# The first phase of a hybrid decoder layer on one Trainium2 core: all five engines in a written order, raw x transposed as it lands, modulation loads in one run

## The chip, the cores and the metric

The kernel runs on one core of a Trainium2 chip. Times are device microseconds (us). An execution's time is a little longer than its span, the stretch that the trace covers. The engines are TensorE (PE; PEld is its weight load), VectorE (DVE), ScalarE (ACT), GpSimd (POOL) and SyncE (SP, which here only issues DMA transfers). Each engine works through its own list of instructions in order; between engines, an instruction waits on semaphores for what it needs.

## The reference

One decoder layer for 256 prompt tokens and 8 sample tokens (264 columns), width 2048. What matters here is its beginning:

```python
mod = jax.nn.silu(c) @ p['w_ada'][l] + p['b_ada'][l]
sh1, sc1, gt1, sh2, sc2, gt2 = jnp.split(mod[:, None, :], 6, axis=-1)
h = rmsnorm(x, p['g_pre_mix'][l]) * (1.0 + sc1) + sh1
z = h @ p['w_in'][l]
(z_uv, hq, hf, hi, hg, gq, gk, gv, gr, glr, z_gate) = jnp.split(z, offsets, axis=-1)
```

`c` has nine rows: one of the prompt and one for each sample token, so the shift `sh1` and the scale `sc1` differ by token. The parts of `z` then feed a gated MLP branch, two gated linear recurrences (one with lower bounds computed from `hg_lb` by exponential and logarithms), a merge, an output product and a squared-ReLU MLP. All weights and data are fp32.

## The kernel before, in words

**Products.** A product of two fp32 tiles is made from three products in a rounded format: each operand is split into a high part `hi` (a cast) and a low part `lo` (operand minus `hi`), and hi·hi, hi·lo and lo·hi are summed in PSUM (lines L602, L603, L604 for the weight products). So each weight tile costs a cast on ACT (`split`, L109, giving `whi`) and a subtraction on DVE (L106, giving `wlo`), and so does each tile of activations.

**The first phase.** `h` lies transposed, 128 channels to a tile, 16 such tiles (k). Tile k needs the rows of `mod` for its channels, which are themselves products over `w_ada`. The phase therefore goes through k in five chunks, `CHUNKS = (2, 2, 4, 4, 4)`, and for each chunk through 20 groups of 256 output channels of `w_in`; partial sums lie in SBUF and each chunk adds to them. The work is cut into granules of 24 weight products with one weight load of 512 KB: in the first two chunks of k a granule has two k and 512 channels, hence two PSUM accumulators (tile `mm`); in the others four k, 256 channels and one accumulator. That makes granules 0 to 9, 10 to 19, 20 to 39, 40 to 59 and 60 to 79. There are two `mm` buffers.

At the end of each granule the accumulators are emptied: in chunk 0 by a copy (`S.copy`, on ACT, L755), later by an addition on DVE (`add`, L103).

**The weight stream.** `granule` takes the next item of `stream`, issues the 24 products, and then calls `stream.ahead()`: this splits the weights of the granule three ahead (two halves: cast, subtraction, cast, subtraction) and starts loads further ahead. Raw weights have four buffers (`RAW_BUFS`, tile `raw`; some pairs use a second kind, `araw`). Split weights have six (`SPLIT_BUFS`, tiles `whi`, `wlo`), two for each granule, so the split of granule g+3 goes into the buffers of granule g. The evictions of the accumulators stand in the program behind the call of `granule`, that is behind this split.

**Modulation.** `First(k0, n)` makes the rows for one chunk: `load` brings batches of `w_ada`; `steps` issues their products (tile `ada`, L274, batches of four in a row); `sums` copies the result (L278); `rows` transposes it (L285), adds the bias (L103) and makes the factor `A1` (L463); then `modulate` makes the tiles (`V.tensor_scalar` L414 or an ACT instruction L416, two small instructions for the 8 sample columns, a cast and a subtraction). The generator `paced` spreads this over the granules of the chunk before.

**The start.** x arrives as two blocks of 128 tokens, in two halves each. `norm_rows` sums the squares, `scale_rows` multiplies the blocks by each token's factor (on ACT and DVE, tokens lie on partitions), and `x_transposed` transposes groups of four 128x128 pieces on TensorE (L241): two groups before the first product, six more between the granules of chunk 0. The lower bounds are written far below in the program.

**Who sets the order.** Between `manual_schedule` and its exit, PE, SP and POOL keep the order in which the code is written. DVE and ACT are ordered by a scheduler from its own estimates.

Of the kernel before, what the change touches and what calls it, by code (L numbers as in the profile page):

```python
# [19 lines left out]
NS = 8  # L20
# [37 lines left out]
def hybrid_step_kernel(  # L58
# [53 lines left out]
    order = tc.manual_schedule(engines={mybir.EngineType.PE, mybir.EngineType.SP, mybir.EngineType.Pool})  # L112
# [103 lines left out]
    def norm_rows(x, xs, xsn, r):  # L216

        ss = tmp([P, 2, 2], "ss0", 1)
        rr = tmp([P, 2 + NS], "rr0", 1)
        junk = blk([P, 1024])  # L220
        for t in range(2):
            for hf in range(2):
                S.activation(junk, x[t][hf], AF.Square, accum_out=ss[:, hf, t:t + 1])
        sq = tmp([P, KT, NS], "sqs", 1)
        mul(sq, xs, xs)
        fold(sq, KT)
        ps = sum_partitions(sq, NS)
        add(ss[:, 0], ss[:, 0], ss[:, 1])
        rstd_small([ss[:, 0], ps], 1.0 / D, rr)
        V.tensor_copy(r, rr[:, 0:2])  # L230
        V.tensor_copy(xx0[:, 0:2], ss[:, 0])
        V.tensor_copy(xx0[:, 2:2 + NS], ps)
        mul(xsn, xs, rr[:, 2:2 + NS].unsqueeze(1).to_broadcast([P, KT, NS]))

    def transposed(x, k):

        ps = sm([P, 2, NP])
        hf, c0 = k // 8, (k % 8) * P
        for i in range(2):
            for t in range(2):  # L240
                T.transpose(ps[:, i, t * P:(t + 1) * P], x[t][hf][:, c0 + i * P:c0 + (i + 1) * P], ident)  # L241
        return ps

    def scale_rows(x, r):
        for hf in range(2):
# [8 lines left out]
    rx = tmp([P, 2], "rx", 1)  # L254
    norm_rows(xt, xsT, xsn, rx)
    xT = []

    def x_transposed(k):

        if k % 4 == 0:  # L260
            xT.append(blk())
        ps = transposed(xt, k)
        dst = xT[k // 4][:, k % 4:k % 4 + 2, 0:NP]
        if k % 4 == 0:
            S.copy(dst, ps)
        else:
            V.tensor_copy(dst, ps)


# [153 lines left out]

    class First:


        def __init__(self, k0, n):
            self.k0, self.n, self.kn = k0, n, 4 // n
            self.nb = KT // self.kn
            self.acc = pada.tile([P, 512], F32, tag="ada", name=nm("ada"))  # L430
            self.w = {}
# [9 lines left out]
        def steps(self, b):  # L441
            w = self.w.pop(b)
            for i in range(self.kn):
                ada_step(self.acc, b * self.kn + i, w[:, i], self.n * 64)
# [4 lines left out]
        def rows(self):  # L449
# [4 lines left out]
            for i in range(ni):  # L454
                for r in range(2):
# [14 lines left out]
            yield  # L470
            for k in range(k0, k0 + n, 2):
                js = slice(k % 4, k % 4 + 2)
                b = xT[q][:, js, :]
                modulate(b, b[:, :, 0:NP], xsn, k, 2, A1, mod[:, 0:KT, :], hh[q][:, js, :], hl[q][:, js, :])
                yield

        def paced(self, count):

            end = count - (5 if count > 9 else 1) - ADA_LEAD
            at = [b * end // self.nb for b in range(self.nb)]  # L480
            b0 = g = 0
            while b0 < self.nb:
                for b in range(self.nb):
                    if at[b] == g:
                        self.load(b)
                if at[b0 + ADA_BATCH - 1] + ADA_LEAD <= g:
                    for b in range(b0, b0 + ADA_BATCH):
                        self.steps(b)
                    b0 += ADA_BATCH
                if b0 == self.nb:  # L490
                    self.sums()
                g += 1
                yield
            yield from self.rows()
# [202 lines left out]
    uT, vF = [blk(), blk()], [blk(), blk()]  # L697
    HQ, HF, HI = ([blk(), blk()] for _ in range(3))
    begin = []
    for g in range(4):  # L700
        begin.append((g * CW, pair(uT[g // 2], g % 2), AF.Gelu_apprx_tanh))
    for g in range(4):
        begin.append((BW + g * CW, pair(vF[g // 2], g % 2), AF.Gelu_apprx_tanh))
    for i in range(2):
        for base, dst, fn in ((2048, HQ, AF.Silu), (3072, HF, None), (4096, HI, None)):
            for g in range(2):
                begin.append((base + 512 * i + g * CW, pair(dst[i], g), fn))
# [15 lines left out]
    first = First(0, CHUNKS[0])  # L723
# [8 lines left out]
    scale_rows(xt, rx)  # L732
    x_transposed(0)
    x_transposed(2)
    for b in (4, 5):
        first.steps(b)
    small_vectors()
    for b in (6, 7):
        first.steps(b)
    first.sums()  # L740
    run(first.rows())
    k0 = 0
    for ci, n in enumerate(CHUNKS):
        final = ci == len(CHUNKS) - 1
        gn = 4 // n
        ng = len(begin) // gn
        if not final:
            nxt = First(k0 + n, CHUNKS[ci + 1]).paced(ng)
        for gi in range(ng):
            accs = [new_acc() for _ in range(gn)]  # L750
            granule(win, 0, n, begin[gi * gn][0], gn * CW, accs, hH, hL, k0, True, True)
            for acc, (c0, dst, fn) in zip(accs, begin[gi * gn:gi * gn + gn]):
                z = acc[:, :, 0:NT]
                if ci == 0:
                    S.copy(dst, z)  # L755
# [4 lines left out]
            if ci == 0 and 2 * gi + 4 < KT:  # L760
                x_transposed(2 * gi + 4)
            if not final:
                next(nxt, None)
            else:
# [5 lines left out]
        if not final:  # L770
            run(nxt)
        k0 += n
    order.__exit__(None, None, None)
# [129 lines left out]
    lnlb, lnom, dlt, oml = (const([P, 8], n) for n in ("lnlb", "lnom", "dlt", "oml"))  # L903

    def lower_bounds():

        lt = [tmp([P, 8], f"lb{i}", 1) for i in range(4)]
        sub(lt[0], lbrawT, lbrawT)
        S.activation(lt[0], lt[0], AF.Exp)
        V.reciprocal(lt[1], lt[0])  # L910
        mul(lt[0], lt[0], lt[1])
        sub(lt[1], lt[0], lt[0])
        V.tensor_scalar(lt[1], lt[1], 0.0, None, ALU.max)
        V.tensor_scalar(lt[2], lt[1], 0.0, -1.0e30, ALU.is_equal, ALU.mult)
        V.tensor_scalar(lt[3], lt[1], 1.0e-19, None, ALU.max)
        S.activation(lnlb, lt[3], AF.Ln)
        add(lnlb, lnlb, lt[2])
        V.tensor_scalar(oml, lt[1], -1.0, 1.0, ALU.mult, ALU.add)
        V.tensor_scalar(lt[3], oml, 1.0e-19, None, ALU.max)
        S.activation(lnom, lt[3], AF.Ln)  # L920
        sub(dlt, lnom, lnlb)

# [19 lines left out]
    def hg_group(i):  # L942
# [8 lines left out]
        def gates():  # L951
            if i == 0:
                lower_bounds()
# [866 lines left out]
```

## Time and profile before

| | |
|---|---|
| median of 3 runs | 1940.19 us (1938.92 to 1940.46) |
| profiled execution | 1938.0 us, span 1935.8 us |
| TensorE busy | 1900.1 us, 98% of the span |
| VectorE, ScalarE, GpSimd busy | 1188.7, 1005.7, 88.0 us |
| mean granted TensorE clock | 0.995 |
| DMA | 442 MB, mean 228 GB/s |

In the rows of the timeline and of the groups, an operation is written as output<-input by the program's names, with its size, its count (x) and in square brackets the idle time of the engine before it and what ended that wait. A row of the view by stretches gives, for each engine, the busy time and the number of instructions (in the order PE, PEld, DVE, ACT, POOL), then the granted clock, the share of DMA engines that were busy, and GB/s.

### The profile page before, as it was taken

To read this page: it belongs to the slowest core of one execution; us is meant where nothing else is said; L and a number is where in the kernel's file an instruction comes from. 1 tells how busy PE (TensorE), PEld (TensorE's weight loads), DVE (VectorE), ACT (ScalarE), POOL (GpSimd) and SP (SyncE) were. 2 spreads that over 40 slices of the span, in tenths; PEclk is the share of its full clock that TensorE was granted. 3 is DMA by queue.
4 is the path that set the end of the run, shared out by engine and by line. 5 is a ranking of instruction groups with operands and counts; after the bars stand their busy time and mean duration, and the time that the engine had idled before them with its cause. 6 is when DMAs were issued, how large, how long until landed. Compare 5 with 4: busy or idle time off the path is not lost. (4 is left out here: it accounts for less than half of the span.)

```text
span 1935.8 us, 42323 instructions
## 1 busy us (share of the span) xinstructions
PE 1900.1 (98%) x17072; PEld 1810.3 (94%) x17072; DVE 1188.7 (61%) x2114; ACT 1005.7 (52%) x1827; POOL 88.0 (5%) x144
## 2 busy tenths in 40 slices
PE   6999999999999999999999999999999999999998
PEld 5989999998999998999999989999999999999997
DVE  4566667686577695565555666545556555555565
ACT  5444354665666765544444566454444545454444
POOL 1000000001101112200000010000000000000000
PEclk9999999999999999999999999999999999999999
DMA  9897787688588788987777846776565555555552
GB/s 314 299 341 250 246 285 216 212 259 277 182 268 280 220 261 277 312 262 250 253 256 231 304 138 191 226 243 191 180 184 178 184 179 181 183 178 185 179 181 100
DMA packets 339381, 442.06 MB, mean 228 GB/s; under 512 B 14931, under 2 KB 281025, under 8 KB 339185
## 3 DMA queue, kind: packets, MB, share of 16 engines
q1 hardware_dynamic: 329120, 409.62, 65.5%
q0 software_dynamic: 8992, 28.48, 4.6%
q8 instruction: 134, 2.20, 0.4%
q10 hardware_dynamic: 1072, 1.25, 0.2%
q14 instruction: 63, 0.51, 0.1%
HBM read 427.60 MB, written 11.70 MB: 227 GB/s over the span
## 5 line engine op out<-in xcount | busy, mean ns | idle before, releaser
L602 PE MATMUL mm<-b,whi 128*128 128x264 f32 x4592 | 1317.2, 287 | 7.6 <-ACT b L109 3.5
L603 PE MATMUL mm<-b,whi 128*128 128x264 f32 x4592 | 1308.6, 285 | 1.9 <-DVE b L106 1.0
L604 PE MATMUL mm<-b,wlo 128*128 128x264 f32 x4592 | 1305.3, 284 | 0.3 <-DVE wlo L106 0.2
L106 DVE TENSOR_TENSOR wlo<-raw,whi 128x512 fp32r<-128x512 f32 x1136 | 776.0, 690 | 570.0 <-ACT whi L109 567.4
L109 ACT CAST whi<-raw 128x512 fp32r<-128x512 f32 x1134 | 693.9, 618 | 726.7 <-PE mm L603 647.9
L602 PEld LDWEIGHTS mm<-b,whi 128*128 128x128 f32 x4592 | 865.8, 189 | 50.2 <-issue 23.8
L603 PEld LDWEIGHTS mm<-b,whi 128*128 128x128 f32 x4592 | 865.8, 189 | 2.6 <-DVE b L106 1.1
L604 PEld LDWEIGHTS mm<-b,wlo 128*128 128x128 f32 x4592 | 866.3, 189 | 1.4 <-DVE wlo L106 0.9
L103 DVE TENSOR_TENSOR b<-b,mm 128x528 f32<-128x528 f32 (+1 forms) x137 | 95.6, 699 | 42.3 <-PE mm L604 42.3
L1057 DVE SCALAR_TENSOR_TENSOR st<-vbc,b,st 128x128 f32<-128x128 f32 (+1 forms) x96 | 34.2, 391 | 52.3 <-DMA vbc<-vs_d 46.8
L1055 ACT ACTIVATE st<-st,fs 128x128 f32<-128x128 f32 (+1 forms) x96 | 37.0, 430 | 51.3 <-DMA st<-in_state_hgrn_dram 26.0
L274 PE MATMUL ada<-b,cT 128*32 128x256 f32 (+1 forms) x640 | 35.4, 361 | 7.4 <-DMA b<-in_w_ada_dram 7.3
L342 PE MATMUL ada<-araw,cT 128*32 128x512 f32 x296 | 39.9, 601 | 0.0
L274 PEld LDWEIGHTS ada<-b,cT 128*32 128x32 f32 x640 | 18.3, 116 | 19.5 <-issue 6.8
L100 DVE TENSOR_TENSOR b<-b,b 128x512 f32<-128x512 f32 (+1 forms) x47 | 34.2, 742 | 1.4 <-ACT b L1165 0.9
L1058 POOL DMA_DIRECT2D out_dram<-st x32 | 23.5, 735 | 153.1 <-DVE st L1057 152.3
L342 PE MATMUL ada<-b,cT 128*32 128x512 f32 x216 | 25.8, 593 | 0.0
L106 DVE TENSOR_TENSOR b<-gt,b 128x528 fp32r<-128x528 f32 x32 | 22.7, 709 | 3.7 <-ACT whi L109 0.5
L106 DVE TENSOR_TENSOR b<-b 128x1024 f32<-128x1024 f32 (+1 forms) x24 | 24.4, 1018 | 0.0
L109 ACT CAST whi<-araw 128x512 fp32r<-128x512 f32 x20 | 12.4, 621 | 20.6 <-PE mm L603 18.1
L100 DVE TENSOR_TENSOR gt<-vt 128x528 f32<-128x528 f32 x32 | 22.4, 701 | 0.9 <-ACT vt L1679 0.9
L1685 ACT ACTIVATE b<-vt 128x528 fp32r<-128x528 f32 x32 | 20.7, 647 | 1.0
(374 smaller groups left out, 872.0 us busy)
## 6 DMA issues: line engine op xcount, KB each, us to landing
raw<-in_w_in_dram SPq DMA_DIRECT2D x232, 512.0 KB, 4.6
raw<-in_w_mlp_up_dram SPq DMA_DIRECT2D x128, 512.0 KB, 3.7
raw<-in_w_mlp_down_dram SPq DMA_DIRECT2D x128, 512.0 KB, 3.6
b<-in_w_ada_dram SPq DMA_DIRECT2D x102, 512.0 KB, 6.5
araw<-in_w_ada_dram SPq DMA_DIRECT2D x74, 512.0 KB, 5.4
raw<-in_w_branch_dram SPq DMA_DIRECT2D x48, 512.0 KB, 4.4
raw<-in_w_out_dram SPq DMA_DIRECT2D x32, 512.0 KB, 4.1
b<-in_w_ada_dram SPq DMA_DIRECT2D x32, 256.0 KB, 5.9
```

Source lines behind the costliest of these rows:

```text
L100: V.tensor_tensor(o, a, b, op=ALU.mult)
L103: V.tensor_tensor(o, a, b, op=ALU.add)
L106: V.tensor_tensor(o, a, b, op=ALU.subtract)
L109: S.copy(hi, src)
L274: T.matmul(acc[32 * j:32 * j + 32, 0:n], cT[:, k, :], w[:, n * j:n * j + n], start=k == 0, stop=k == KT - 1)
L342: T.matmul(self.acc[32 * j:32 * j + 32, :], cT[:, k, :], ws[j // 2][:, j % 2 * 512:j % 2 * 512 + 512], start=k == 0, stop=k == KT - 1)
L602: T.matmul(o, a, xh(k + j), start=first and j == 0, stop=False)
L603: T.matmul(o, a, xl(k + j), start=False, stop=False)
L604: T.matmul(o, b, xh(k + j), start=False, stop=last and j == n - 1)
L1055: S.activation(st[:, i, :], st[:, i, :], AF.Copy, scale=fs[:, h0 + i, b:b + 1])
L1057: V.scalar_tensor_tensor(st[:, i, :], v[:, i, :], k[:, h0 + i, NP + b:NP + b + 1], st[:, i, :], ALU.mult, ALU.add)
L1058: nc.gpsimd.dma_start(G.s_out(b, h0, nh), st)
```

## The change

The change rewrites the first phase so that DVE and ACT, too, keep the written order. In detail:

- The list of engines in `manual_schedule` gains DVE and ACT.
- Raw x is transposed block by block as it lands (`x_block`, 32 transposes, all ahead of the first product). The token factors come later: two products of a matrix of ones with a diagonal matrix of factors spread them over all partitions (`row_factors`), and four DVE products 128x1024 scale the transposed x.
- The lower bounds move to behind granule 24, the constants of the later phases (two loads, 0.42 MB) to behind granule 22. Where these loads were, three batches of the second chunk's `w_ada` stand (six loads of 256 KB).
- The generator `paced` goes. A table says behind which granule each batch of products, the sums, the rows and each pair of tiles stand: batches of four behind granules 4 and 7; 9, 11, 14, 17; 25, 28, 31, 34; 45, 48, 51, 54; the rows and first tiles one granule after the last batch. The `w_ada` loads are spread over the granules.
- In chunk 0 the second accumulator is copied by DVE, the first by ACT (both L815).
- At the first tile (`modulate_first`) POOL makes the sample columns and DVE all prompt columns; POOL also makes the first weight subtraction.
- Blocks for the results are taken when they are first written.

```diff
-    order = tc.manual_schedule(engines={mybir.EngineType.PE, mybir.EngineType.SP, mybir.EngineType.Pool})
+    order = tc.manual_schedule(engines={mybir.EngineType.PE, mybir.EngineType.SP, mybir.EngineType.Pool, mybir.EngineType.DVE, mybir.EngineType.Activation})
...
-    norm_rows(xt, xsT, xsn, rx)
...
-        ps = transposed(xt, k)
...
-    def scale_rows(x, r):
-        for hf in range(2):
-            S.activation(x[0][hf], x[0][hf], AF.Copy, scale=r[:, 0:1])
-            V.tensor_scalar(x[1][hf], x[1][hf], r[:, 1:2], None, ALU.mult)
...
+    def x_block(t, hf):
+        S.activation(junk, xt[t][hf], AF.Square, accum_out=ss0[:, hf, t:t + 1])
+        for q in (2 * hf, 2 * hf + 1):
...
+            for j in range(4):
+                c0 = (4 * (q % 2) + j) * P
+                T.transpose(ps[:, j, :], xt[t][hf][:, c0:c0 + P], ident)
...
+    for t in range(2):
+        V.tensor_scalar(dg[:, t, 0:P], ident, rr0[:, t:t + 1], None, ALU.mult)
...
+    def row_factors():
+        ps = sm([P, 2, P])
+        for t in range(2):
+            T.matmul(ps[:, t, :], ones, dg[:, t, 0:P], start=True, stop=True)
+        rb = tmp([P, 2, NT], "vt")
+        S.copy(rb[:, 0, 0:NP].rearrange("p (t n) -> p t n", t=2), ps)
+        for q in range(4):
+            x = xT[q][:, :, 0:NP]
+            mul(x, x, rb[:, 0:1, 0:NP].to_broadcast([P, 4, NP]))
...
+    def modulate_first(b, xs, A, B, hi, lo):
+        d = b[:, :, NP:NT]
+        G = nc.gpsimd
+        G.tensor_tensor(d, xs[:, 0:2, :], A[:, 0:2, 1:NC], op=ALU.mult)
+        G.tensor_tensor(d, d, B[:, 0:2, 1:NC], op=ALU.add)
...
-    def paced(self, count):
...
-    nc.sync.dma_start(cst[:, 256:904], consts[:, 256:904])
-    nc.sync.dma_start(msk, masks.rearrange("p (l t) -> p l t", l=6))
-    for b in range(4):
+    for b in range(3):
+        firsts[1].load(b)
...
+    raw, hi, lo = halves[0]
+    nc.gpsimd.tensor_tensor(lo, raw, hi.bitcast(F32), op=ALU.subtract)
+    first.rows()
+    first.tiles(0)
...
+    at_batches(1, (4, 7))
+    at_batches(2, (9, 11, 14, 17))
...
+    at(22, rest)
+    at(24, lower_bounds)
...
                 if ci == 0:
-                    S.copy(dst, z)
+                    (V.tensor_copy if a else S.copy)(dst, z)
                 else:
                     add(dst, dst, z)
...
-            if ci == 0 and 2 * gi + 4 < KT:
-                x_transposed(2 * gi + 4)
...
+            for fn, args in acts.pop(gg, ()):
+                fn(*args)
```

What this does to the order on three engines (`mm_`, `b_`, `raw_`, `whi_` and `wlo_` with a number are single buffers in their turn):

ACT in chunk 0, between the first granules, before. `L755` copies an accumulator `mm`, `L109` casts a half of a later granule's weights, `L265` copies transposed x:

```order
L109 CAST whi_426<-raw_341 128x512
L109 CAST whi_430<-raw_341 128x512
L755 COPY b_167<-mm_400 128x528
L755 COPY b_167<-mm_401 128x528
L109 CAST whi_482<-raw_343 128x512
L109 CAST whi_486<-raw_343 128x512
L755 COPY b_168<-mm_456 128x528
L755 COPY b_168<-mm_457 128x528
L265 COPY b_494<-sm_495 128x2x256
L755 COPY b_169<-mm_501 128x528
L109 CAST whi_527<-raw_377 128x512
L109 CAST whi_531<-raw_377 128x512
```

And now, in the same place:

```order
L109 CAST whi_416<-raw_386 128x512
L109 CAST whi_420<-raw_386 128x512
L815 COPY b_426<-mm_368 128x528
L109 CAST whi_458<-raw_388 128x512
L109 CAST whi_462<-raw_388 128x512
L815 COPY b_468<-mm_432 128x528
L109 CAST whi_500<-raw_390 128x512
L109 CAST whi_504<-raw_390 128x512
L815 COPY b_510<-mm_474 128x528
```

Before, two casts stood ahead of the copies in the first granules, and later the copy of the first accumulator stood ahead of the casts; now two casts stand ahead of the copy in each granule, and one of the two copies has gone to DVE.

DVE in chunk 1 before, where `L103` adds an accumulator to the sums and `L106` subtracts for a later granule's weights:

```order
L103 TENSOR_TENSOR b_166<-b_166,mm_864 128x528
L106 TENSOR_TENSOR wlo_891<-raw_783,whi_890 128x512
L103 TENSOR_TENSOR b_166<-b_166,mm_865 128x528
L106 TENSOR_TENSOR wlo_895<-raw_783,whi_894 128x512
L103 TENSOR_TENSOR b_167<-b_167,mm_918 128x528
L106 TENSOR_TENSOR wlo_945<-raw_821,whi_944 128x512
L103 TENSOR_TENSOR b_167<-b_167,mm_919 128x528
L106 TENSOR_TENSOR wlo_949<-raw_821,whi_948 128x512
```

And now:

```order
L106 TENSOR_TENSOR wlo_933<-raw_751,whi_932 128x512
L106 TENSOR_TENSOR wlo_937<-raw_751,whi_936 128x512
L103 TENSOR_TENSOR b_426<-b_426,mm_906 128x528
L103 TENSOR_TENSOR b_426<-b_426,mm_907 128x528
L106 TENSOR_TENSOR wlo_973<-raw_828,whi_972 128x512
L106 TENSOR_TENSOR wlo_977<-raw_828,whi_976 128x512
L103 TENSOR_TENSOR b_468<-b_468,mm_946 128x528
L103 TENSOR_TENSOR b_468<-b_468,mm_947 128x528
```

The adds stood alternately with the subtractions and now stand in pairs behind both.

ACT at the start before, from the copy of the first transposed x to the casts of the first tile (`lb`, `lnlb`, `lnom`: the lower bounds; `gt`: the modulation sums):

```order
L265 COPY b_245<-sm_246 128x2x256
L909 ACT_TABLE_LOAD
L909 ACTIVATE lb_815_4677<-lb_815_4677 128x8
L278 COPY gt_295<-ada_176 128x128
L916 ACT_TABLE_LOAD
L916 ACTIVATE lnlb<-lb_818_4680 128x8
L920 ACTIVATE lnom<-lb_818_4680 128x8
L416 ACTIVATE b_245<-b_245,mod,A_165 128x256
L109 CAST whi_315<-raw_201 128x512
L109 CAST b_302<-b_245 128x264 x2
```

And now:

```order
L266 COPY vt_292<-sm_289 128x256
L279 COPY gt_343<-ada_264 128x128
L761 CAST whi_345<-raw_249 128x512
L761 CAST whi_348<-raw_249 128x512
L109 CAST b_357<-b_143 128x264 x2
```

The lower bounds with their table loads and ACT's share of the first tile are gone from here, and both weight casts stand ahead of the first tile's. POOL has this in the same place, where it had nothing (`L429` and `L430` make the sample columns):

```order
L764 ISA
L764 TENSOR_TENSOR wlo_346<-raw_249,whi_345 128x512
L429 TENSOR_TENSOR b_143<-xsn_128,A_220 128x2x8
L430 TENSOR_TENSOR b_143<-b_143,mod 128x2x8
L1024 DMA b_3866<-in_gla_w_up_dram 16x512
```

The sample columns stand behind the weight subtraction on POOL.

More of the change, by code (lines that the diff above doesn't have):

```diff
@@ L422, in hybrid_step_kernel @@
     A1 = const([P, KT, NC], "A1")
+    def modulate_first(b, xs, A, B, hi, lo):
[3 more added lines that the diff above has]
+        G.tensor_tensor(d, d, B[:, 0:2, 1:NC], op=ALU.add)
+        for j in range(2):
+            V.tensor_scalar(b[:, j, 0:NP], b[:, j, 0:NP], A[:, j, 0:1], B[:, j, 0:1], ALU.mult, ALU.add)
+        for j in range(2):
+            split(b[:, j, :], hi[:, j, :], lo[:, j, :])
     class First:
@@ L429, in __init__ @@
             self.nb = KT // self.kn
-            self.acc = pada.tile([P, 512], F32, tag="ada", name=nm("ada"))
+            self.acc = None
             self.w = {}
@@ L441, in steps @@
         def steps(self, b):
+            if b == 0:
+                self.acc = pada.tile([P, 512], F32, tag="ada", name=nm("ada"))
             w = self.w.pop(b)
@@ L454, in rows @@
             for i in range(ni):
-                for r in range(2):
+                for r in (1, 0):
                     cs = slice(r * KT + k0, r * KT + k0 + n)
@@ L469, in rows, with tiles @@
                 hl.append(blk(dt=F32R))
[L470 to L473, printed above, removed]
-                modulate(b, b[:, :, 0:NP], xsn, k, 2, A1, mod[:, 0:KT, :], hh[q][:, js, :], hl[q][:, js, :])
-                yield
-        def paced(self, count):
[L479 to L494, printed above, removed]
+        def tiles(self, k):
+            q, js = k // 4, slice(k % 4, k % 4 + 2)
+            b = xT[q][:, js, :]
+            if k == 0:
+                modulate_first(b, xsn, A1, mod[:, 0:KT, :], hh[q][:, js, :], hl[q][:, js, :])
+            else:
+                modulate(b, b[:, :, 0:NP], xsn, k, 2, A1, mod[:, 0:KT, :], hh[q][:, js, :], hl[q][:, js, :])
     rate = [0.0, 0.0]
@@ L901, in hybrid_step_kernel @@
     bg.g.append(gen_a)
[L903 to L921, printed above, removed]
     def log_sigmoid(out, z, a):
```

155 lines of the change are left out of this document (96 added, 59 removed).

## Prediction

> **What bounds the kernel now.** I read the page first, then the products by stage, then what TensorE waited for, then the timeline at the places where it waited. The page:
>
> ```profile
> span 1935.8 us, 42323 instructions
> PE 1900.1 (98%) x17072; PEld 1810.3 (94%) x17072; DVE 1188.7 (61%) x2114; ACT 1005.7 (52%) x1827; POOL 88.0 (5%) x144
> ```
>
> TensorE is the bound, so a wait of TensorE costs its full length and work taken from it is worth its full length. The change touches the time up to the end of the first 80 granules. A granule is 24 products; granules 0 to 9 (chunk 0) and 10 to 19 (chunk 1) fill two PSUM accumulators each, the later ones one. The next view counts the products (tile mm) by stage: granules 1 to 9, 10 to 19, 20 to 39, and 60 to 79.
>
> ```profile
> 34.13:68.99 34.86, 27.88 (x216) 26.83 (x217) 0.00 (x0) 10.41 (x18) 1.00 0.81 267
> 68.99:111.75 42.76, 32.71 (x242) 31.27 (x241) 13.23 (x19) 0.59 (x1) 0.96 0.99 370
> 111.75:179.20 67.45, 59.83 (x482) 58.60 (x481) 14.06 (x20) 0.00 (x0) 1.00 0.78 264
> 246.20:309.20 63.00, 59.30 (x482) 58.44 (x481) 14.07 (x20) 0.00 (x0) 1.00 0.87 285
> ```
>
> Twenty granules without trouble take 63.0 us, ten should take 31.5 and their modulation products; granules 10 to 19 take 42.76. The waits of TensorE over the whole run say what there is to gain:
>
> ```profile
> PE ada L274 <- DMA b<-in_w_ada_dram: 7.3, 3, 6.3
> PE mm L602 <- DVE b L103: 2.7, 2, 2.0
> PE mm L602 <- ACT b L755: 1.3, 2, 0.6
> ```
>
> The first is w_ada landing before there is other work. The other two are waits of a product for an accumulator to be emptied, by ACT (L755) and by DVE (L103). They are few, and the change meets just these.
>
> **Part 1: evictions behind casts, granules 1 to 9.** This is the timeline around the first ACT wait: the first product of granule 1, the casts of the weights of a later granule, the last product of granule 1, four transposes, the two copies, the first product of granule 2.
>
> ```profile
> 34.14 0.37 PE L602 MATMUL mm<-b,whi 128*128 128x264 f32 x1
> ...
> 36.51 1.35 ACT L109 CAST whi<-raw 128x512 fp32r<-128x512 f32 x2 [0.40 <-PE mm L603]
> 37.04 0.29 PE L604 MATMUL mm<-b,wlo 128*128 128x264 f32 x1
> 37.17 0.60 PE L241 MATMUL sm<-cst,b 128*128 128x128 f32 x4
> 37.77 1.09 ACT L755 COPY b<-mm 128x528 f32<-128x528 f32 x2
> 38.41 0.39 PE L602 MATMUL mm<-b,whi 128*128 128x264 f32 x1 [0.65 <-ACT b L755]
> ```
>
> The casts wait for products of the granule that runs (L603), since their buffers are that granule's: there are six, two a granule, and the split is three granules ahead. The second cast can only end about 0.7 us after the granule. ACT works in order; the copies stand behind the casts, and the next granule's first accumulator stands behind the first copy. Without the transposes TensorE could have gone on at 37.17 (0.12 after 37.04); it went on at 38.41, so this order costs 1.24 us, and here the transposes fill half of it. Before, ACT has this order in granules 1 and 2 alone; from granule 3 on the copy stands ahead. The new order has it in every granule of chunk 0: cast, cast, copy. A granule lasts 37.17 - 34.14 = 3.03, with the wait 4.27.
>
> A run of modulation products between two granules covers the wait:
>
> ```profile
> 85.62 0.28 PE L604 MATMUL mm<-b,wlo 128*128 128x264 f32 x1
> 85.84 1.93 PE L274 MATMUL ada<-b,cT 128*32 128x256 f32 x32
> 87.70 0.39 PE L602 MATMUL mm<-b,whi 128*128 128x264 f32 x1
> ...
> 90.64 0.28 PE L604 MATMUL mm<-b,wlo 128*128 128x264 f32 x1
> ```
>
> It costs 87.70 - 85.74 = 1.96, and in chunk 1 a granule lasts 90.76 - 87.70 = 3.06. After the change such runs follow granules 4, 7 and 9. From granule 1 to granule 10: 6 x 4.27 + 3 x (3.03 + 1.96) = 40.6 us, where 34.86 were: **+5.7**. The six groups of transposes that leave this stage (about 0.45 each, 2.7) are in this sum: they no longer fill the waits.
>
> **Part 2: adds behind subtractions, granules 10 to 19.** Here DVE adds both accumulators to the sums. This is the one place where before has the order that the change gives to all ten granules: cast, cast; subtraction, subtraction; add, add.
>
> ```profile
> 104.39 1.36 ACT L109 CAST whi<-raw 128x512 fp32r<-128x512 f32 x2 [1.34 <-PE mm L603]
> 104.93 0.28 PE L604 MATMUL mm<-b,wlo 128*128 128x264 f32 x1
> 105.04 1.43 DVE L106 TENSOR_TENSOR wlo<-raw,whi 128x512 fp32r<-128x512 f32 x2
> 106.39 1.31 DVE L103 TENSOR_TENSOR b<-b,mm 128x528 f32<-128x528 f32 x2
> 107.23 0.37 PE L602 MATMUL mm<-b,whi 128*128 128x264 f32 x1 [2.02 <-DVE b L103]
> ```
>
> TensorE could have gone on at 105.05 and went on at 107.23: 2.18 us. It is longer than part 1's because the second subtraction follows the second cast and the add follows it. In before's other granules the add stands between the two subtractions and no wait is seen. Now a granule takes 3.06 + 2.18 = 5.24 whether a modulation run (1.96, shorter) stands behind it or not: 10 x 5.24 = 52.4 for 42.76, **+9.6**. At granule 18 the new tiles' work, ahead of the next adds on DVE, adds some 0.5 (rows below).
>
> **Part 3: the start.** The last transpose of the modulation rows, a table load of the lower bounds, the casts of the first tile, the first product; two POOL groups of the page; the issue of the fourth weight load and its size and latency; and the DMA rate meanwhile (last number, GB/s):
>
> ```profile
> 24.58 0.33 PE L285 MATMUL sm<-cst,gt 128*128 128x128 f32 x1 [0.39 <-ACT gt L278]
> 24.55 1.28 ACT L916 ACT_TABLE_LOAD   x1
> 27.97 0.72 ACT L109 CAST b<-b 128x264 fp32r<-128x264 f32 x2
> 28.43 0.59 PE L602 MATMUL mm<-b,whi 128*128 128x264 f32 x1 [3.52 <-ACT b L109]
> ...
> L1575 POOL TENSOR_TENSOR b<-b,b 128x512 f32<-128x512 f32 x1 | 1.3, 1280 | 0.0
> L1595 POOL TENSOR_TENSOR b<-xsn,b 128x32 fp32r<-128x32 f32 x4 | 1.5, 375 | 0.3
> ...
> 22.30 0.38 SPq L562 DMA_DIRECT2D raw<-in_w_in_dram  x1
> raw<-in_w_in_dram SPq DMA_DIRECT2D x1, 512.0 KB, 7.9
> ...
> 27.00:28.00 1.00, 0.00 (x0) 0.00 (x0) 0.48 (x3) 1.00 (x3) 0.00 (x0) 0.50 1.06 401
> ```
>
> The rows are there at 24.9. The lower bounds, with a table load of 1.28 just there, leave this place, so the factor A1 can be ready at about 25.6. But POOL now makes the sample columns, and its two instructions stand behind its new weight subtraction: that needs the weight's cast (about 26.1), takes 1.28 by the 128x512 row, then twice 0.375: 28.15. One cast of 0.36 and a hand-over: first product at 28.7, where 28.43 was. The freed table load is worth nothing, since POOL's chain fills it.
>
> The fourth weight load landed at 22.30 + 7.9 = 30.2. Six batch halves of 256 KB (1.57 MB) now stand ahead of it and 0.42 MB of constants no longer: 1.15 MB more at 400 GB/s is 2.9 us, so it lands at 33.1. Its two casts stand on ACT ahead of granule 0's copy: 33.1 + 2 x 0.6 + 0.6 = 34.9, granule 1 at 34.95 for 34.14: **+0.8**. Without that lateness the order of part 1 gives the same: a granule 0 that ends at 33.7 and 1.24 more.
>
> Costed at nothing: the 32 transposes of raw x at the start, since x lands while TensorE has nothing else (its wait for w_ada above is 7.3 us) and w_ada sets the rows' time; the two products with ones, as short and as early. The four DVE products 128x1024 that scale x cost 1.02 us each by the nearest row,
>
> ```profile
> L106 DVE TENSOR_TENSOR b<-b 128x1024 f32<-128x1024 f32 (+1 forms) x24 | 24.4, 1018 | 0.0
> ```
>
> and if a broadcast operand makes one half as long again, 6 us: from about 17.7 to 23.6, still ahead of 24.9. If that cover went, the first tile would be late by the rest, 1 us at most. The lower bounds at granule 24 cost DVE some 2 us and ACT two table loads in a stage where one accumulator is filled while the other is emptied; a granule of 3 us is the slack. The constants at granule 22 and the spread w_ada loads use a DMA that is not full there (264 GB/s in the row of granules 20 to 39). SP waits, as before, for weight buffers that DVE frees; DVE's waits are for TensorE, so SP's loads slip with it and no sooner.
>
> **Part 4: tiles ahead of adds, granules 35 to 39 and 55 to 59.** Pieces of a tile, on DVE:
>
> ```profile
> 168.76 0.42 DVE L103 TENSOR_TENSOR mod<-sm,vec 128x18 f32<-128x18 f32 x4
> 170.45 0.41 DVE L414 TENSOR_SCALAR b<-b,A,mod 128x256 f32<-128x256 f32 x1
> 171.99 0.70 DVE L106 TENSOR_TENSOR b<-b,b 128x528 fp32r<-128x528 f32 x1
> ```
>
> Before, weight subtractions and adds are strewn among these. In the fixed order all of it stands between the add of granule 35 and the subtractions of the next split. From the end of granule 35: last cast and subtraction 1.46 (part 2's rows), add 0.66, rows 0.42 and 0.2, sample columns and tile 0.75, cast 0.63, subtraction 0.70: 4.9; the two subtractions of granule 39's weights and the add of granule 36: 6.9. Two granules of TensorE take 6.3 to 6.4, so granule 38 waits 0.55; the second tile pair, a granule later, makes the next wait some 1.1. Two stages: 2 x 1.7 = **+3.4**. By the same rows the smaller tiles at granules 18 and 20 cost about 0.5 each: **+1.0**.
>
> **Part 5: the clock.** What followed the wait of 2.02 us in part 2 (the last three numbers are clock, DMA share, GB/s):
>
> ```profile
> 104.00:108.00 4.00, 1.98 (x16) 1.79 (x16) 3.96 (x13) 2.24 (x4) 0.00 (x0) 1.00 0.84 273
> 108.00:111.50 3.50, 3.50 (x18) 3.50 (x17) 2.20 (x8) 1.78 (x3) 0.00 (x0) 0.51 1.03 391
> ```
>
> In the 3.5 us after it the granted clock was 0.51 and 18 products ran. The steady pace (482 products in 59.30 us, 0.123 each) gives 28.5; the 10.5 missing are 1.3 us. In chunk 1 the new order gives such a wait after every granule; runs of modulation products break three of them, seven stay. I take the clock's choice as one by fixed stretches of time in which too little ran, and a wait of 2.0 us fell there wholly into one; of seven at 5.24 us apart I let half do so: 3.5 x 1.3 = **+4.6**, with ends of 0 and 18 (each wait and the stretch after it slowed). The waits of part 1 are 1.24 and I cost them nothing: the one at 37.17 is followed by no slower product (0.39, 0.37 each at the first).
>
> [...]
>
> **The sum.** 0.8 + 5.7 + 9.6 + 1.0 + 3.4 + 4.6 = 25.1 us. All of it lies on TensorE's path ahead of granule 60; behind it the program is the same and only shifts. The profiled execution was 1938.0 (span 1935.8), 2.2 below the median of 1940.19: 1963.1 for a like execution, about **1965** for the median.
>
> **Rivals.**
>
> *The clock isn't cut by these waits.* Each wait leaves over a third of any 3.4 us stretch filled, and the slow stretch at 108.00 is one case only, so it might come of something else. Sum 20.5: about 1960.5. Chance 0.20. [...]
>
> *The clock is cut at nearly every wait.* If seven waits with both neighbouring stretches lose 2 x 1.3 each, the clock costs 18 rather than 4.6: 1979; the stretches would then be slow through all of chunk 1. Chance 0.13.
>
> *Faster.* The fixed order puts the evictions where TensorE never waits for them. The transposes (2.7), both waits seen (1.3) and the hole in granules 10 to 19 are then won: 42.76 against 10 x 3.06 and four runs of 1.96 = 38.4, 4.3 us; less 0.8 at the start, 7.5: about 1932.5. It decides whether the second cast ends 1.24 us or more before the granule's end. It would, were the split's buffers those of an earlier granule; the casts' waits on L603 in parts 1 and 2 speak against that. Chance 0.09.
>
> *No change.* Only ACT's order bites, since DVE's adds find the subtractions done: +5.7 and +0.8 less the 4.3: 1942. The row of 105.04 speaks against it. Chance 0.03.
>
> **How the numbers follow.** The main case has 0.55. Its own range is 1957 to 1975 (clock 0 to 14, tiles 0 to 5). The range has to hold 8 in 10 and so takes in the case without the clock with terms up to 8 lower, and the lower half of the case with the full clock: 1952 to 1978. A measurement of this kernel tells about 0.2% (3.9 us) from no change: faster 0.09, same 0.03, slower 0.88.
>
> **What the profile after would show.** The first product near 28.7; granule 1, 10 and 20 at 34.95, 75.5 and 128.4 (the first two sums; the third with the tiles and half of the clock's loss); the waits for ACT's copy at about 1.1 to 1.2 us a granule up to 75, those for DVE's adds at 2.0 to 2.2 up to 128; stretches of clock 0.5 in chunk 1 alone; shorter waits near granules 38, 39, 58 and 59; granule 80 at about 334 for 309.2; no transposes between the products after the first; no wait at granule 24. The prediction is wrong if the casts and subtractions of the split end well ahead of the granule's end in the new order, if the copies or adds run ahead of them, or if the waits stay and the clock does what neither end allows.

## The result, and the profile after

The changed kernel takes 1971.87 us (median of 4 runs, 1968.51 to 1975.11) where the kernel before takes 1940.33: a ratio of 1.016, 95% interval 1.0147 to 1.0173. It is slower by 31.5 us. The forecast was 1965, 1952 to 1978. The profiled execution of the changed kernel took 1974.0, its span is in the page:

```profile
span 1972.2 us, 42411 instructions
PE 1913.0 (97%) x17076; PEld 1820.9 (92%) x17076; DVE 1201.5 (61%) x2128; ACT 995.3 (50%) x1813; POOL 89.7 (5%) x147
```

The view by stretches, for granules 1 to 9, 10 to 19, 20 to 39 and 60 to 79 (all instructions, so the counts hold the modulation products too; the first number after the stretch is its length, and behind the engines stand clock, DMA share and GB/s):

```profile
35.36:75.83 40.47, 34.08 (x377) 31.03 (x377) 20.15 (x36) 17.04 (x30) 0.00 (x0) 1.00 0.88 284
75.83:133.48 57.65, 43.43 (x342) 38.55 (x339) 27.57 (x50) 14.44 (x24) 0.00 (x0) 0.88 0.61 204
133.48:203.50 70.02, 68.79 (x610) 64.15 (x611) 44.61 (x87) 30.08 (x50) 0.00 (x0) 0.98 0.74 254
271.80:334.90 63.10, 63.10 (x514) 59.17 (x513) 39.93 (x67) 32.80 (x54) 0.00 (x0) 1.00 0.89 288
```

Granules 10 to 19 stand out: TensorE is busy for 43.43 of 57.65 us, at a mean clock of 0.88, and the DMA rate is the lowest of the four, 204 GB/s, since loads wait for buffers (the load queue waited 42.8 us of the stage for weight subtractions). Stage by stage, in the two profiled executions; "behind the phase" is the time from the begin of granule 80 to the end of the last product into `mm`:

| | before | after | difference | forecast |
|---|---|---|---|---|
| granule 1 begins | 34.14 | 35.36 | +1.2 | +0.8 |
| granules 1 to 9 | 34.85 | 40.48 | +5.6 | +5.7 |
| granules 10 to 19 | 42.76 | 57.65 | +14.9 | +14.7 (9.6, 0.5, 4.6) |
| granules 20 to 39 | 67.47 | 70.04 | +2.6 | +2.2 (0.5, 1.7) |
| granules 40 to 59 | 67.04 | 68.30 | +1.3 | +1.7 |
| granules 60 to 79 | 63.01 | 63.07 | +0.1 | 0 |
| behind the phase | 1620.5 | 1630.7 | +10.2 | 0 |

The waits of TensorE over the whole run:

```profile
PE mm L599 <- DVE b L103: 15.4, 9, 2.0
PE mm L599 <- ACT b L815: 7.4, 7, 1.1
...
PE sm L630 <- issue: 2.4, 1, 2.4
PE mm L600 <- issue: 2.0, 1, 2.0
PE mm L599 <- issue: 1.8, 1, 1.8
...
PE mm L601 <- DVE wlo L106: 1.0, 1, 1.0
```

The first two rows are the forecast's: 2.7 and 1.3 us before, 15.4 and 7.4 now. The three rows with "issue", a wait for nothing that the profile shows, are new, and they lie behind the phase. So does the last, a wait for the low part of a weight (0.2 before). In chunk 0 a granule now ends like this (casts, last products, the copy, the next granule):

```profile
37.72 1.34 ACT L109 CAST whi<-raw 128x512 fp32r<-128x512 f32 x2 [2.41 <-PE mm L600]
...
38.96 0.59 ACT L815 COPY b<-mm 128x528 f32<-128x528 f32 x1
39.61 0.39 PE L599 MATMUL mm<-b,whi 128*128 128x264 f32 x1 [1.08 <-ACT b L815]
```

and in chunk 1 like this:

```profile
78.21 1.35 ACT L109 CAST whi<-raw 128x512 fp32r<-128x512 f32 x2 [3.13 <-PE mm L600]
...
78.75 0.28 PE L601 MATMUL mm<-b,wlo 128*128 128x264 f32 x1
78.86 1.43 DVE L106 TENSOR_TENSOR wlo<-raw,whi 128x512 fp32r<-128x512 f32 x2 [2.87 <-ACT whi L109]
80.21 1.31 DVE L103 TENSOR_TENSOR b<-b,mm 128x528 f32<-128x528 f32 x2
81.05 0.36 PE L599 MATMUL mm<-b,whi 128*128 128x264 f32 x1 [2.02 <-DVE b L103]
```

From 78.75 to 81.05 are 2.30 us, less the 0.12 of one product 2.18: the same chain and the same length as the one case before showed.

The clock, in five stretches of 3.4 us, laid by the two at half clock, which begin at 82.49 and 116.62 and last 3.41:

```profile
79.10:82.50 3.40, 1.45 (x12) 1.48 (x13) 2.38 (x4) 0.47 (x1) 0.00 (x0) 1.00 0.67 195
82.50:85.90 3.40, 3.40 (x23) 2.93 (x25) 0.69 (x1) 1.21 (x2) 0.00 (x0) 0.50 1.04 392
109.80:113.20 3.40, 1.97 (x16) 2.00 (x17) 1.90 (x3) 0.00 (x0) 0.00 (x0) 1.00 1.05 404
113.20:116.60 3.40, 1.38 (x11) 1.20 (x11) 2.33 (x4) 1.24 (x2) 0.00 (x0) 1.00 0.52 200
116.60:120.00 3.40, 3.40 (x17) 3.40 (x17) 0.28 (x1) 0.00 (x0) 0.00 (x0) 0.50 0.57 159
```

The wait from 78.87 to 81.05 lies in the first stretch but for 0.2 us, and the second runs at 0.50. The wait at 109 was cut by the border at 109.8, 0.7 us on one side and 1.4 on the other, and what follows runs at 1.00. The wait at 114.2 lies wholly in a stretch again, and 116.6 to 120.0 runs at 0.50.

### The profile page after: what moved, and what is told of

The parts are those of the page before. It is cut to its first block, busy times and chain, and to the rows that moved or that the text cites. A ratio compares the mean times of both kernels' runs of the same rounds, so it can differ in the third digit from the quotient of the medians.

```text
span 1972.2 us, 42411 instructions
## 1 busy us (share of the span) xinstructions
PE 1913.0 (97%) x17076; PEld 1820.9 (92%) x17076; DVE 1201.5 (61%) x2128; ACT 995.3 (50%) x1813; POOL 89.7 (5%) x147
## 5 line engine op out<-in xcount | busy, mean ns | idle before, releaser
L599 PE MATMUL mm<-b,whi 128*128 128x264 f32 x4592 | 1325.2, 289 | 28.7 <-DVE b L103 15.4
L106 DVE TENSOR_TENSOR wlo<-raw,whi 128x512 fp32r<-128x512 f32 x1135 | 775.7, 691 | 615.1 <-ACT whi L109 609.4
L109 ACT CAST whi<-raw 128x512 fp32r<-128x512 f32 x1132 | 691.6, 618 | 767.7 <-PE mm L600 694.0
L103 DVE TENSOR_TENSOR b<-b,mm 128x528 f32<-128x528 f32 (+1 forms) x137 | 94.5, 696 | 16.6 <-PE mm L601 16.6
L275 PEld LDWEIGHTS ada<-b,cT 128*32 128x32 f32 x640 | 17.4, 112 | 16.5 <-DMA b<-in_w_ada_dram 7.8
L106 DVE TENSOR_TENSOR b<-gt,b 128x528 fp32r<-128x528 f32 x32 | 22.7, 708 | 3.4
L106 DVE TENSOR_TENSOR b<-b 128x1024 f32<-128x1024 f32 (+1 forms) x24 | 24.4, 1022 | 0.0
L343 PEld LDWEIGHTS ada<-b,cT 128*32 128x32 f32 x216 | 6.9, 110 | 15.1 <-issue 14.6
```

The lines of the kernel that those rows point to most:

```text
L103: V.tensor_tensor(o, a, b, op=ALU.add)
L106: V.tensor_tensor(o, a, b, op=ALU.subtract)
L109: S.copy(hi, src)
L275: T.matmul(acc[32 * j:32 * j + 32, 0:n], cT[:, k, :], w[:, n * j:n * j + n], start=k == 0, stop=k == KT - 1)
L343: T.matmul(self.acc[32 * j:32 * j + 32, :], cT[:, k, :], ws[j // 2][:, j % 2 * 512:j % 2 * 512 + 512], start=k == 0, stop=k == KT - 1)
L599: T.matmul(o, a, xh(k + j), start=first and j == 0, stop=False)
```

## The experiments

Nine further runs were made, one of them of the changed kernel again. "Phase" is the begin of granule 80, in the profile.

**The evictions ahead of the split.** In the changed kernel, in all chunks, `granule` (its new argument is `ahead`) no longer ends with the split; the split stands behind the evictions:

```diff
-        stream[0].ahead()
+        if ahead:
+            stream[0].ahead()
...
+            late = True
+            granule(win, 0, n, begin[gi * gn][0], gn * CW, accs, hH, hL, k0, True, True, not late)
...
+            if late:
+                stream[0].ahead()
             for fn, args in acts.pop(gg, ()):
```

> The changed kernel, but in all five chunks the evictions (copies, adds) are issued ahead of the split of later weights; everything else, the fixed order too, stays. Theory A (evictions stand behind the split's casts and subtractions): the waits for L815 and L103 go; granule 10 begins near 68.5 us (now 75.8), granule 20 near 107.5 (now 133.5), granule 80 near 307 (now 334.9); the median falls by 26 to 28 to about 1944 to 1946, and by some 5 more if what the changed kernel loses behind the phase goes too. Rival B (weights or modulation rows arrive too late, whatever the order): the waits change their name but granule 20 stays later than 125, median above 1960.

Measured: 1937.23 us, ratio to before 0.9982 (0.9972 to 0.9992). The stages 1 to 9 and 10 to 19:

```profile
34.41:66.83 32.42, 32.42 (x379) 30.67 (x378) 19.23 (x35) 18.18 (x32) 0.00 (x0) 1.00 1.01 346
66.83:105.03 38.20, 35.97 (x342) 32.58 (x339) 27.14 (x50) 14.72 (x25) 0.00 (x0) 1.00 0.89 306
```

40.5 became 32.4 and 57.7 became 38.2; TensorE is busy without a gap in the first. Phase 306.5 for 334.9, and what was lost behind the phase is gone too (1620.8). Theory A holds: not the written order as such costs the time, but the place of the evictions in it. With the evictions there, the change as a whole is a small gain, 4.0 us. The time fell further than the 26 to 28, or some 33, that were expected: 34.6.

**The same in granules 10 to 19 alone.** (`late = ci == 1`.)

> The changed kernel with the evictions ahead of the split in granules 10 to 19 alone. Theory A: granules 10 to 19 take 38.5 to 39.5 us for 57.7, of which about 13 is waits and 5 to 6 the clock; the stage before it stays at 40.5; median about 1953. If the slow stretches of the clock come of something else than the waits, about 44 us and 1958. Rival B: little change.

Measured: 1951.42 us, ratio 1.0057 (1.0043 to 1.0071). Granules 1 to 9 take 40.50, granules 10 to 19 38.17 at clock 1.00. The waits and the clock of chunk 1 are thus worth 19.5 us of the phase; the forecast had 9.6 and 0.5 for the waits, 4.6 for the clock, and 4.3 for the hole of before, 19.0.

**The order alone, without the rest of the change.** The kernel before with one line:

```diff
-    order = tc.manual_schedule(engines={mybir.EngineType.PE, mybir.EngineType.SP, mybir.EngineType.Pool})
+    order = tc.manual_schedule(engines={mybir.EngineType.PE, mybir.EngineType.SP, mybir.EngineType.Pool, mybir.EngineType.DVE, mybir.EngineType.Activation})
```

> The kernel before with one line of the change: DVE and ACT are added to the engines in written order; all other code as before. Theory A (the order alone costs the time): granules 1 to 9 take about 40.5 us for 34.85, granules 10 to 19 52 to 58 for 42.8, median 1960 to 1968. Rival B (the moved loads, tiles and transposes cost it, and the order matters only with them): median below 1950.

Measured: 1968.21 us, ratio 1.0141 (1.0126 to 1.0155). Granules 1 to 9 take 40.91, granules 10 to 19 59.49 at a mean clock of 0.86:

```profile
35.63:76.54 40.91, 34.74 (x365) 32.45 (x365) 15.95 (x29) 22.99 (x43) 0.00 (x0) 1.00 0.68 227
76.54:136.03 59.49, 46.99 (x370) 41.41 (x371) 27.67 (x50) 14.84 (x25) 0.00 (x0) 0.86 0.75 272
```

So this one line makes 27.6 of the 31.5 us. Its phase ends at 337.5, 28.3 later than before's and later than the changed kernel's 334.9: inside the phase the rest of the change gains 2.6 us. The changed kernel is slower all the same, since it loses more behind the phase (1630.7 for 1622). The stage of granules 10 to 19 is longer than the 52 to 58 us expected; all six of its waits were followed by a stretch of half clock. Here the six groups of transposes still lie between the granules of chunk 0, and the stage takes as long (40.91 for 40.48): they run inside the waits.

**The rest of the change, without the order.** The changed kernel with DVE and ACT left to the scheduler (the line above in reverse).

> The changed kernel with ACT and DVE left to the scheduler again (PE, SP and POOL in written order, as before the change). Theory A: the scheduler puts most evictions ahead of the casts and alternates adds and subtractions again, so the waits go; the lower bounds stand at the start again and the first tile's casts behind all weight casts, so the first product comes at 30 to 32; granule 20 near 112, median 1945 to 1950. Rival B (the other parts of the change cost the time): median stays at 1965 or more.

Measured: 1940.57 us, ratio 0.9999 (0.999 to 1.0008). Granules 1 to 9 take 34.41, granules 10 to 19 37.48; the first product comes at 30.9 and granule 1 at 37.13, 3.0 later than before, as the lower bounds and the weights' casts stand ahead of the first tile again. Phase 307.3, 2.0 less than before; behind it the profile shows 1626.2, 5.7 more. The median is below the 1945 to 1950 that were expected, and granule 20 began at 109.0, not 112.

**The waits filled, first attempt.** To see whether the waits cost the clock, 14 products whose result is not used were put behind seven granules of chunk 1.

> The changed kernel with 14 more products, whose result is not used, behind the granules 10 to 19 that have no modulation products: they fill 1.7 of each wait of 2.2 us. Theory C (a wait of 2.2 us brings a stretch of half clock): granules 10 to 19 keep their waits for L103 but have no slow stretch, and take 52 to 53 us for 57.7; median about 1967. Rival (the slow stretches come of something else, such as the load on the power supply or the DMA): the same slow stretches, 57 to 58 us, median 1972; if the added products cost more than the waits hide, above 1972.

Measured: 1977.56 us, ratio 1.0192 (1.0178 to 1.0206); granules 10 to 19 took 67.53. The expectation was wrong, and by a slip in the experiment: the added products read a weight half, so the cast into its buffer waited for them too, and the whole chain cast, subtraction, add began later: TensorE's waits for the adds came to 16.3 us over the run, for 15.4 without the added products. It shows what the chain hangs on, the last product that reads the weights. Of the clock it says little, although it had two slow stretches in this stage.

**The waits filled, with x alone.** The same, but the added products read only tiles of x:

```diff
+        if fill:
+            ps = sm()
+            for _ in range(fill):
+                T.matmul(ps[:, 0:NT], xh(k)[:, 0:P], xh(k), start=True, stop=True)
         stream[0].ahead()
```

> As fill_c1, but the 14 unused products behind granules 10, 12, 13, 15, 16, 18 and 19 read only the tiles of x, not the weights whose buffer the next cast waits for. Theory C (a wait of about 2.2 us brings a stretch of half clock): no slow stretch in granules 10 to 19, which take 52 to 53 us for 57.7 in the changed kernel; end of the phase near 330 for 334.9. Rival (the slow stretches come of something else): four or five slow stretches as in the changed kernel and 57 to 58 us.

Measured: 1959.37 us, ratio 1.0096 (1.0083 to 1.0109). No slow stretch in granules 10 to 19:

```profile
75.85:127.67 51.82, 49.32 (x440) 44.65 (x437) 27.56 (x50) 14.46 (x24) 0.00 (x0) 1.00 0.68 228
```

With 98 products more the stage is 5.8 us shorter. The granules still begin when the adds are done (six waits for them are left, 0.3 us at most); only the clock stays, at 1.00 for 0.88. So 5.8 us of the stage were the clock's, and theory C holds here. The granules of the changed kernel say the same: those that a slow stretch met, 11, 13, 14 and 17, took 6.45, 6.71, 6.70 and 6.70 us, the other six of the stage 5.16 to 5.21, together 5.8 us more; with the waits filled all ten took 5.15 to 5.22. The phase ends at 328.7 for 334.9. The remaining gain of the median, 12.5 - 6.2 = 6.3 us, comes from behind the phase (1622.6 for 1630.7); of this below.

**POOL takes subtractions.** evict_first keeps one wait of 2.2 us, ahead of granule 20, and two slow stretches behind it. DVE there (start, duration, engine):

```profile
101.51 0.42 DVE L103 TENSOR_TENSOR mod<-sm,vec 128x18 f32<-128x18 f32 x4
102.90 0.63 ACT L109 CAST b<-b 128x528 fp32r<-128x528 f32 x1 [0.18 <-DVE b L415]
103.56 0.71 DVE L106 TENSOR_TENSOR b<-b,b 128x528 fp32r<-128x528 f32 x1 [0.74 <-ACT b L109]
104.19 1.31 DVE L103 TENSOR_TENSOR b<-b,mm 128x528 f32<-128x528 f32 x2
105.03 0.36 PE L599 MATMUL mm<-b,whi 128*128 128x264 f32 x1 [2.23 <-DVE b L103]
```

The tile of granule 18 stands ahead of the adds of granule 19. The first attempt gave POOL the weight subtractions behind granules 17 to 19.

> evict_first, and the six weight subtractions issued behind granules 17, 18 and 19 made by POOL, so that DVE reaches the adds of granule 19 sooner. Expected: the wait of 2.2 us ahead of granule 20 falls to 0.5 to 1.2 and the two slow stretches behind it go; granules 20 to 39 take 68 us for 71.2; median 1934 for 1937.2. Rival (POOL's subtractions of 1.3 us each make weights late or slow DVE): no gain or a loss, 1937 to 1942.

Measured: 1935.94 us, ratio 0.9982 (0.9972 to 0.9993), the same as evict_first's; granules 20 to 39 took 71.28 again. The expectation failed and its rival held. The rows say why:

```profile
99.13 2.54 POOL L571 TENSOR_TENSOR wlo<-raw,whi 128x512 fp32r<-128x512 f32 x2 [2.46 <-PE mm L605]
99.29 0.70 DVE L103 TENSOR_TENSOR b<-b,mm 128x528 f32<-128x528 f32 x1 [0.76 <-PE mm L606]
100.51 1.20 DVE L100 TENSOR_TENSOR b<-xsn,A 128x16 f32<-128x16 f32 x1
...
103.55 2.51 POOL L571 TENSOR_TENSOR wlo<-araw,whi 128x512 fp32r<-128x512 f32 x2 [1.88 <-ACT whi L570]
104.84 1.26 DVE L100 TENSOR_TENSOR b<-xsn,A 128x16 f32<-128x16 f32 x1
```

A DVE product of 128x16, 0.17 us in evict_first, took 1.20 and 1.26, and ended both times 0.04 us after POOL's pair of subtractions (101.67 and 106.06). The add from PSUM beside it kept its 0.70. Of what POOL took from DVE, DVE lost 1.03 us in the first of these products (1.20 for 0.17), and the wait ahead of granule 20 is 2.05 us where evict_first has 2.23. That the product waited for POOL is an estimate from these ends; how the one held up the other was not shown.

**The tile taken apart.** evict_first, with the subtraction of the tile between the two adds of granule 19, the next tile's columns there too, and the split of that granule held back:

```diff
+                if gg == 19 and a == 0:
+                    firsts[2].tiles_b(4)
+                    firsts[2].tiles_a(6)
+            if gg == 19:
+                firsts[2].tiles_b(6)
+                stream[0].hold = False
...
+            if gg == 18:
+                firsts[2].tiles_a(4)
+                stream[0].hold = True
```

> evict_first, with the first tiles of the third chunk (behind granules 18 and 19) taken apart: the subtraction of the first pair and the columns of the second stand between the two adds of granule 19, and the split of granule 21's weights waits until behind granule 19. If the 2.2 us ahead of granule 20 come of the tile's chain ahead of the adds on DVE: that wait falls below 1 us, the two slow stretches at 105 go, granules 20 to 39 take 67.5 to 68.5 us for 71.2, median about 1933. If the delayed split makes the weights of granules 21 and 22 late instead: a new wait for wlo there and no gain, 1936 to 1939.

Measured: 1932.91 us, ratio 0.9965 (0.9951 to 0.9978), the best of all. The add now comes first:

```profile
101.01 0.69 DVE L103 TENSOR_TENSOR b<-b,mm 128x528 f32<-128x528 f32 x1
101.17 0.63 ACT L502 CAST b<-b 128x528 fp32r<-128x528 f32 x1 [0.18 <-DVE b L500]
101.71 0.60 ACT L501 ACTIVATE b<-b,mod,A 128x256 f32<-128x256 f32 x1
101.84 0.71 DVE L106 TENSOR_TENSOR b<-b,b 128x528 fp32r<-128x528 f32 x1
```

The wait ahead of granule 20 is gone, two of 0.2 and 0.4 us for the tiles' low parts are left, no stretch there is slow, granules 10 to 19 take 35.81 and 20 to 39 68.45, and the phase ends at 300.8, 8.5 us before that of the kernel before. The median gains only 6.2 us, since 1623.7 us lie behind the phase, 3.2 more than before.

**The changed kernel once more,** for the loss behind the phase.

> The changed kernel once more, for a second profile. If the loss of 10 us behind the phase belongs to this program's place in memory, TensorE waits again for about 2 us near its matrix instructions 3750, 4133, 5411 and 7996 (counted from its first), each with a transfer of instructions beginning there; if it is chance, in other places or not at all. Granule 80 again near 335, median 1970 to 1974.

Measured: 1973.89 us, ratio 1.0165 (1.0147 to 1.0182), phase 335.5, and 1634.5 behind it. TensorE waits again near its instructions 3750, 4133 and 5411, for 2.60, 2.05 and 2.75 us from one instruction to the next; the fourth place shows nothing this time. In the first profile the wait at that fourth place is the one for the low part of a weight, whose subtraction ended at 852.88; the product began at 852.97. The other three have no such cause in the profile. The first of them, in the first profile of the changed kernel:

```profile
453.17 0.22 PE L630 MATMUL sm<-b 128*32 128x32 f32 x2 [2.38 <-issue]
```

and in the view of the DMA queues of those 3 us one transfer of 16 KB, on the queue that the view calls "instruction", which begins at 450.8, as TensorE stops:

```profile
q8 instruction: 1, 0.02, 2.2%
```

There are 134 such transfers in the run, and 135 in the two kernels with 98 products more. In evict_first, whose TensorE runs the same instructions in the same order, such a transfer begins 0.2 us ahead of instruction 3750, and TensorE does not wait there. Three other kernels do wait near these places; their rows, of evict_first_c1, sched_act_dve and evict_first_tiles in turn:

```profile
PE mm L600 <- issue: 3.5, 2, 2.0
PE mm L600 <- issue: 2.6, 2, 1.9
PE mm L617 <- issue: 1.1, 1, 1.1
```

Their time behind the phase, 1626.0, 1626.2 and 1623.7, is longer than before's as well. The kernels that lost little there (evict_first, evict_first_pool and the two with added products: 1620 to 1623 us) have waits of 0.5 us at most at these places or none, and order_only, with waits of about 1.2 and 1.6 at two of them, no more than 1622. The eleven profiles hold sixteen waits of 0.3 us or more that are put down to "issue". Fifteen of them end 2.2 to 2.6 us after such a transfer began, and the sixteenth 3.0 us after one that took 1.50 us and not about 1. In those fifteen the time from the transfer's begin thus varied little, while the sixteen waits were 0.3 to 2.5 us long. That the waits are for these transfers is an estimate from this timing and was not shown: no run changed the transfers. Why they begin where they do stays open.

## Why the prediction was right, and where it was not

- **Parts 1 and 2, the waits.** Right. The rows of granules that had the order before gave the price of all: 5.6 for 5.7 in chunk 0, and 2.18 us a granule in chunk 1. (That no wait is seen in before's other granules of chunk 1 was misread: one of 0.7 us, ahead of granule 18, is the second of the two in the row of 2.7.) order_only shows that the order makes them, evict_first that the place of the evictions does.
- **Part 3, the start.** The first product came at 28.43, not 28.7 (POOL's two small instructions took 0.25 each, not 0.375). Granule 1 came 1.2 later, not 0.8: the fourth weight's cast began at 33.44 on landing, 0.3 later than worked out. Granule 0, worked out to end at 33.7, ended at 34.0: it ran at half clock to its end (0.50 up to 34.7; before, up to 33.0), which the forecast did not look at. The four products that scale x took 4.63 us, 17.47 to 22.10, where up to 6 were allowed for.
- **Part 4, the tiles.** Right in size for granules 35 to 39 and 55 to 59: waits of 0.65 and 0.9 us in each of the two stages, 1.55 for 1.65. The 0.5 us at granule 18 do not show: the waits ahead of granules 19 and 20 are 1.95 and 2.18, no longer than the others. Granule 20 took 4.51 us for 3.64 before; part of this is the slow stretch behind 133.5, since it took 4.07 in fill_x_c1, which has none there.
- **Part 5, the clock.** Slow stretches followed these waits, as forecast, and the price was too low. The fixed stretches of time, which the forecast took from one case (in before's trace the half clock begins at 108.07 and lasts 3.41), show in the profile after: slow stretches that begin whole multiples of 3.41 us apart, four in chunk 1 and a fifth at its end, for three and a half; the filled waits put the clock's share of the stage at 5.8 us for 4.6. In the profiles of the changed kernel (two) and of order_only, 20 such waits lie in chunk 1. Where 1.9 us or more of a wait fell into one stretch of the 3.4 us grid, the next stretch was slow, each time; where the border left 1.8 or less on either side, none was. order_only had all six of its waits inside. The limit is not sharp: in the profile of fill_c1 two waits with 1.9 and 2.0 us inside one stretch were not followed by a slow one. In evict_first a wait of 0.8 us inside a stretch that was already slow was followed by a second.
- **The sum.** 25.1 forecast, 25.6 in the profile, up to the end of the phase. That it is so close is partly luck: in granules 10 to 19 the clock cost 5.8 for 4.6, and the waits and the tile 9.1 for 10.1. The 128.4 given for the begin of granule 20 holds the waits and the tiles alone, though it is said to hold half of the clock's loss; with all of the sum's terms it is 133.0, and 133.49 was measured.
- **The step that failed: "behind it the program is the same and only shifts".** It is the same, yet it took 10.2 us longer in the profile. The three waits put down to "issue" make 6.5 of it (2.57, 2.06 and 2.26 from one instruction to the next, less 0.12 each), the one for the low part of a weight 1.2, and slow stretches at 454 and 615 follow two of them. Against the median it is 31.5 less 25.6, about 6. The median lies 7 us above the forecast, and the range held because it was wide.
- **The rival "faster".** Its mechanism was right, for another kernel: with the evictions ahead of the split the phase is 2.8 us shorter than before, and 8.5 with the tile apart. Its price, 7.5 us, left out the tile ahead of granule 20 and its clock.

## What to carry to other kernels

On an engine with a fixed order, an instruction that empties an accumulator should stand ahead of work that waits for the same products to end; a scheduler had done that here in most granules without being told. When an order is written by hand, look in the profile for one place where the new order already exists and price it there. In this kernel a wait of 2 us on TensorE cost another 1.3 to 1.5 us in clock where a slow stretch followed it (granules of 6.45 to 6.71 us for 5.16 to 5.21), so filling it with products that read nothing of the chain may pay (5.8 us of granules 10 to 19 here), and removing it pays twice (19.5 us).

## What the runs showed of the hardware that was not expected

The slow stretches of the clock lay on a grid of 3.41 us: in the first profile of the changed kernel they begin at 82.49, 92.73, 99.56, 116.62 and 133.69, whole multiples of it apart, and last 3.41 each. Whether one followed a wait went with the wait's place on the grid in all 20 waits of three profiles (1.9 us or more inside one stretch, or 1.8 or less), though not in two of fill_c1, and two executions of one kernel differed (four and three slow stretches between 75 and 133 us; granules 10 to 19 took 57.65 and 55.98). TensorE was idle for 1.8 to 2.5 us near the same three places in two profiles of one kernel, each time beside a transfer on the "instruction" queue, and for 0.5 us at most in evict_first with the same list; it went on 2.2 to 2.6 us after the transfer began. DVE's 128x16 products took up to 1.1 us longer while POOL subtracted (1.26 for 0.17), while its add from PSUM kept its 0.70.
